# A hybrid attention and HGRN layer: down-weight differences formed beside the up tiles, a tile of their own for the meta rows, ScalarE first at query and key banks, three first-stage banks

## The chip, the cores and the metric

The kernel runs on one core of a Trainium2 chip, in one launch. The metric is the device time of that launch in microseconds (us). The engines of the core work from queues of their own: TensorE (PE; its weight loads are PEld), VectorE (DVE), ScalarE (ACT), GpSimd (POOL) and SyncE (SP), which only issues transfers here.

## The reference

One decoder layer over 1024 tokens with 16 meta tokens ahead of them (1040 rows), width 1024, in float32. Two kinds of heads work side by side on the same input, four differential-attention heads and four HGRN2 heads; a convolutional feed-forward layer follows.

```python
a = rmsnorm(h, ln_mix_pre[l])
proj = a @ w_in[l]
dq, dk, dv, hq, hf, hi, hg = jnp.split(proj, SPLITS, axis=-1)
...
y_diff = diff_attention(dq, dk, dv, diff_lambda[l], diff_subln[l], rel_bias_table, lam_init)
y_hgrn = hgrn2(hq, hf, hi, hg, lb_all[l], hgrn_gnorm[l])
mix = jnp.concatenate([y_diff, y_hgrn], axis=-1) @ w_out[l]
h = h + rmsnorm(mix, ln_mix_post[l])
a = rmsnorm(h, ln_ffn_pre[l])
y = conv_ffn(a, w_ffn_up[l], ffn_conv_w[l], ffn_conv_b[l], w_ffn_down[l])
h = h + rmsnorm(y, ln_ffn_post[l])
```

`conv_ffn` multiplies by a 1024 x 5632 matrix, convolves each of the 5632 channels over three tokens, multiplies gelu of one half by the other half and multiplies by a 2816 x 1024 matrix. The meta rows are dropped from the output.

## The kernel before

Every float32 operand of a large matmul is split into a high part (rounded to the matmul's input type) and a low part (the rest), and each product is three matmuls: high x high, high x low, low x high. `split` (L146) makes the parts: a ScalarE cast, then a subtraction on VectorE or GpSimd.

The order of TensorE's instructions is the order of the program (`manual_schedule`, L104). On the other engines, and on SyncE's queue of transfers, a planner orders the instructions: among those whose inputs its model of the time finds ready, it takes the one that comes first in the program. So an operation can be put far ahead of its place in the text when nothing holds it back. `issue_after(x)` keeps an operation behind x on x's engine, and while `state["ordered"]` is set (L792 to L907) the other engines keep program order too. A tile with a tag takes one of the tag's buffers; a further tile of the tag waits until a buffer is released.

The stages, in order of time:

1. **First stage** (L756 to L923, about the first 60 us). Nine blocks of rows are normed, transposed on TensorE and stored as `ahi` and `alo`. Between the transposes stand the query, key and value projections of head 0, for three groups of blocks (`GROUPS`, L31). `head0_first` (L849) gives the matmuls of the first group piece by piece, `block` (L889) transposes one block, `far_block` (L838) prepares one. PSUM has 8 banks: two with the tag `ip`, six with the tag `m` (`deep`, L110). `bias_tables` (L304) forms the lambda term `nlam` and then the bias tables of the four heads.
2. **Heads** (L935 to L940). For each head, `interleave` (L59) mixes two streams: the HGRN projections (`dense`, L742) with attention (`attn`), then the next head's query, key and value projections with the HGRN recurrence (`hgrn_head`). A projection group ends in an evacuation: `ev_q` (L594) and `ev_k` (L599) write a query or key bank as high part in one half of the partitions and low part or a copy in the other. `flush` (L391) transposes value tiles that an earlier group left; `dense` calls it in step 8 of the 24 of a group. `dense` also draws one step of `down_sums` (L184) per group: it loads four 128x512 blocks of the down weights for each of 11 row blocks, forms four differences on VectorE (S11 = W12 - W11, S12 = W22 - W12, S22 = W22 - S11, S21 = W21 - S22, in place) and stores them in the scratch array `tsc`. The tiles have the tag `wd`, six buffers of the pool `wdsums`.
3. **Output projection and norms** (L942 to L1253). Its first half of the columns is made beside the last HGRN head, its second half in a loop over blocks (L1218). `post` (L1131) of a block loads its residual rows `xh` (two buffers), adds the normed output, stores the sum in `hsc` and norms it again; `trans(i - 2)` transposes an earlier block on TensorE. The meta rows are block 0: their `xh` is also what `trans(0)` reads, in iteration 4.
4. **Up projections** (L1339 to L1372). For 22 column tiles `ft`, each with two halves of the tokens, the 2 x 2 block product is made from seven products in place of eight (`unit`, L1298: steps j = 0 to 6). After j = 1, the addition `u2` reads the bank pb, into which step 3 accumulates further. `gated` (L1272) convolves on ScalarE and VectorE, multiplies on GpSimd and stores a tile in `gsc`. `prep` (L1083) makes the weights' sums and parts for the next tile, from tiles `ra`.
5. **Down projection** (L1374 to L1547). The same seven-product scheme; four of its weight operands are the differences that lie in `tsc` (L1397), the others come from the weights themselves. Its operands from `gsc` are loaded into tiles with the tag `gk` (L1390), four buffers of the pool `down`, which opens at L1359, ahead of the up tiles.

Of the kernel before, what the change touches and what calls it, by code (L numbers as in the profile page):

```python
# [33 lines left out]
FA, FH, FO = 840, 800, 740  # L34

# [50 lines left out]
def layer_kernel(ctx: ExitStack, tc: tile.TileContext, x, meta, table, lbl, gpre, gpost, win,  # L86
# [23 lines left out]
    deep = {"ip": 2, "m": 6}  # L110
# [73 lines left out]
    def down_sums():  # L184
        def load(k):
            with tc.issue_after(last_load[-1].ins):
                for nm, kk, half in (("11", k, 0), ("12", k, 1), ("22", k + NF // 2, 1), ("21", k + NF // 2, 0)):
                    b[nm] = wsp.tile([P, 512], F32, tag="wd", name=f"wd{nm}_{k}")
                    SY.dma_start(b[nm], wdown[P * kk: P * (kk + 1), 512 * half: 512 * (half + 1)])

        b = {}
        load(0)
        yield
        yield
        for k in range(NF // 2):
            for j, d, p_, q_ in ((0, "11", "12", "11"), (2, "12", "22", "12"), (1, "22", "22", "11"), (3, "21", "21", "22")):
                V.tensor_tensor(b[d], b[p_], b[q_], op=ALU.subtract)
                with tc.issue_after(last_load[-1].ins):
                    SY.dma_start(tsc[j][P * k: P * (k + 1)], b[d])
                yield  # L200
            if k + 1 < NF // 2:
                load(k + 1)
                yield

    wd_sums = down_sums()
# [98 lines left out]
    def bias_tables():  # L304
# [8 lines left out]
        V.tensor_scalar(nlam, nlam, -(0.8 - 0.6 * math.exp(0.0)), None, ALU.add)  # L313
        oh = zp.tile([32, 384], F32, tag="oh", name="oh", bufs=1)
# [270 lines left out]
    def attn_in(h):  # L585
# [299 lines left out]
    def ahead_of(n):  # L885
        for _ in range(n):
            next(first_group)
# [726 lines left out]
```

## Time and profile before

| | us |
|---|---|
| three timed runs | 1338.4, 1341.98, 1343.84 |
| their median | 1341.98 |
| the profiled execution | 1336.17 |
| its span, first to last instruction | 1334.1 |
| busy ScalarE | 692.0 |
| busy GpSimd | 432.3 |

The profile is of one execution. All work of an engine that goes through the wrapper at L45 to L56 carries the line L53, so such instructions are known by their tiles: `u<-pb,x` is an operation that writes u from pb and x. Matmul durations overlap, since TensorE is pipelined; what counts is the distance from one start to the next. In a list of instructions in order of time, the columns are the start, the time taken, the engine, the line, the operation, the tiles, the shapes, and in brackets the idle time before it with what ended that.

### The profile page before, as it was taken

To read this page: it belongs to the slowest core of one execution; us is meant where nothing else is said; L and a number is where in the kernel's file an instruction comes from. 1 tells how busy PE (TensorE), PEld (TensorE's weight loads), DVE (VectorE), ACT (ScalarE), POOL (GpSimd) and SP (SyncE) were. 2 spreads that over 40 slices of the span, in tenths; PEclk is the share of its full clock that TensorE was granted. 3 is DMA by queue.
4 is the path that set the end of the run, shared out by engine and by line. 5 is a ranking of instruction groups with operands and counts; after the bars stand their busy time and mean duration, and the time that the engine had idled before them with its cause. 6 is when DMAs were issued, how large, how long until landed. Compare 5 with 4: busy or idle time off the path is not lost.

```text
span 1334.1 us, 26146 instructions
## 1 busy us (share of the span) xinstructions
PE 1287.9 (97%) x10172; PEld 1187.0 (89%) x10172; DVE 911.1 (68%) x1531; ACT 692.0 (52%) x1635; POOL 432.3 (32%) x340
## 2 busy tenths in 40 slices
PE   7999999999999999998998999999999999999997
PEld 6899899989999998677888999999999998878875
DVE  7675657475746574647797687787787776697586
ACT  8465356535654665246665445444445444454453
POOL 5211212121212110334055666666666630010121
PEclk9999999999999999999999999999999999999999
DMA  5331343144311223686412222223222226954253
GB/s 208 123 129 62 116 153 116 56 141 134 111 56 54 82 85 127 194 258 230 144 54 83 95 88 72 74 94 103 87 81 72 82 86 211 326 181 166 88 205 118
DMA packets 99425, 164.99 MB, mean 124 GB/s; under 512 B 10035, under 2 KB 34899, under 8 KB 99302
## 3 DMA queue, kind: packets, MB, share of 16 engines
q1 hardware_dynamic: 99302, 163.32, 35.9%
q8 instruction: 80, 1.31, 0.4%
q14 instruction: 43, 0.35, 0.1%
HBM read 122.65 MB, written 40.63 MB: 122 GB/s over the span
## 4 chain that ended last, share of the span: by engine, by line
PE 46%; DVE 7%; issue 3%; ACT 3%; DMA 2%; POOL 2%; SPq 0%; DVEq 0%; POOLq 0%; ACTq 0%
PE pd L1460 5%; PE pd L1461 5%; PE pd L1459 5%; PE pb L1309 4%; PE pb L1311 4%; PE pb L1310 4%; PE pc L1309 2%; PE pa L1309 2%; PE pa L1311 2%; PE pa L1310 2%; PE pc L1310 2%; PE pc L1311 2%; PE py L982 1%; PE py L980 1%; PE py L978 1%
## 5 line engine op out<-in xcount | busy, mean ns | idle before, releaser
L1309 PE MATMUL pb<-t,uh 128*128 128x258 f32 x504 | 142.9, 284 | 7.7 <-DVE u L53 7.7
L1310 PE MATMUL pb<-t,uh 128*128 128x258 f32 x504 | 141.7, 281 | 0.0
L1311 PE MATMUL pb<-t,ul 128*128 128x258 f32 x504 | 141.5, 281 | 0.0
L1460 PE MATMUL pd<-wl,gh 128*128 128x512 f32 x308 | 122.0, 396 | 0.3 <-DVE wl L53 0.2
L1459 PE MATMUL pd<-wh,gh 128*128 128x512 f32 x308 | 121.6, 395 | 0.0
L1461 PE MATMUL pd<-wh,gl 128*128 128x512 f32 x308 | 121.6, 395 | 0.0
L53 DVE SCALAR_TENSOR_TENSOR c<-uu,cwt,c 128x514 f32<-128x514 f32 (+1 forms) x88 | 97.1, 1104 | 20.6 <-ACT c L53 19.9
L1309 PEld LDWEIGHTS pb<-t,uh 128*128 128x128 f32 x504 | 95.4, 189 | 9.2 <-DVE u L53 8.9
L53 POOL TENSOR_TENSOR c<-c,c 128x514 f32<-128x514 f32 (+1 forms) x44 | 63.4, 1441 | 122.6 <-ACT c L53 118.5
L1310 PEld LDWEIGHTS pb<-t,uh 128*128 128x128 f32 x504 | 95.5, 189 | 0.0
L1311 PEld LDWEIGHTS pb<-t,ul 128*128 128x128 f32 x504 | 95.2, 189 | 0.0
L1309 PE MATMUL pa<-t,uh 128*128 128x258 f32 (+1 forms) x336 | 95.2, 283 | 0.0
L1311 PE MATMUL pa<-t,ul 128*128 128x258 f32 (+1 forms) x336 | 95.0, 283 | 0.0
L1310 PE MATMUL pa<-t,uh 128*128 128x258 f32 (+1 forms) x336 | 94.8, 282 | 0.0
L1309 PE MATMUL pc<-t,uh 128*128 128x258 f32 (+1 forms) x336 | 94.4, 281 | 0.0
L1310 PE MATMUL pc<-t,uh 128*128 128x258 f32 (+1 forms) x336 | 94.0, 280 | 0.0
L1311 PE MATMUL pc<-t,ul 128*128 128x258 f32 (+1 forms) x336 | 93.7, 279 | 0.0
L53 DVE SCALAR_TENSOR_TENSOR c<-ug,cwt,c 128x514 f32<-128x514 f32 (+1 forms) x88 | 86.7, 986 | 2.0 <-ACT c L53 1.4
L53 POOL TENSOR_TENSOR ul<-ws,uh 128x512 fp32r<-128x512 f32 x42 | 61.0, 1453 | 41.1 <-ACT uh L53 36.6
L1460 PEld LDWEIGHTS pd<-wl,gh 128*128 128x128 f32 x308 | 57.7, 187 | 15.5 <-DVE wl L53 1.6
L1459 PEld LDWEIGHTS pd<-wh,gh 128*128 128x128 f32 x308 | 57.7, 187 | 14.1
L1461 PEld LDWEIGHTS pd<-wh,gl 128*128 128x128 f32 x308 | 57.7, 187 | 14.0
(372 smaller groups left out, 4119.4 us busy)
## 6 DMA issues: line engine op xcount, KB each, us to landing
ra<-in_wup_dram SPq DMA_DIRECT2D x88, 256.0 KB, 2.6
mp<-msc SPq DMA_DIRECT2D x23, 512.0 KB, 6.3
wd<-in_wdown_dram SPq DMA_DIRECT2D x44, 256.0 KB, 4.4
tsc<-wd SPq DMA_DIRECT2D x44, 256.0 KB, 2.8
wi<-tsc SPq DMA_DIRECT2D x44, 256.0 KB, 2.8
gi<-gsc SPq DMA_DIRECT2D x33, 256.0 KB, 3.9
wi<-in_wdown_dram SPq DMA_DIRECT2D x33, 256.0 KB, 3.2
gsc<-c SPq DMA_DIRECT2D x22, 257.0 KB, 2.1
```

The lines of the kernel that those rows point to most:

```text
L53: ins = call(*args, **kw)
L978: T.matmul(py[:r], mh, hi, start=(first and k == ks[0]), stop=False)
L980: T.matmul(py[:r], mh, lo, start=False, stop=False)
L982: T.matmul(py[:r], ml, hi, start=False, stop=(last and k == ks[-1]))
L1309: T.matmul(pt, hi[:, s], th[:, k], start=(first and k == 0), stop=False, skip_group_check=True)
L1310: T.matmul(pt, hi[:, s], tl[:, k], start=False, stop=False, skip_group_check=True)
L1311: T.matmul(pt, lo[:, s], th[:, k], start=False, stop=(k == 3), skip_group_check=True)
L1459: T.matmul(py, gh[:, s], wh, start=(k == 0 and pr not in (3, 7)), stop=False, skip_group_check=True)
L1460: T.matmul(py, gh[:, s], wl, start=False, stop=False, skip_group_check=True)
L1461: T.matmul(py, gl[:, s], wh, start=False, stop=(k == NH - 1), skip_group_check=True)
```

## The change

It has these parts:

- `down_sums` moves from the projections to the up tiles, into the pool `down` with the tag `gk`. From tile 6 on (`SUMS`) it is drawn once after each of the steps j = 1, 3, 5 and 6, behind the newest addition that reads a bank of `unit` (`marks["last"]`). Its loads have no such tie.
- `xh` of the meta rows goes into the tile e0 of the pool `early`, and the loads of `xh` are issued one block earlier, after the loads of the next block's operands.
- `ev_q` and `ev_k`: ScalarE's reads of a bank come first, then VectorE's; the copy of the key's high part to the other partitions reads the copy in SBUF, not the bank.
- `flush` in `dense` at step 14, not 8.
- First stage: three `ip` banks and five `m` banks. The first group's matmuls are written out by kind; the query bank is evacuated after block 4, the key bank after block 5, and the query bank of the second group is filled between the value parts. The second value weights are split after block 3. The lambda term goes behind the last `alo` part, together with the small tables.

```diff
-    deep = {"ip": 2, "m": 6}
+    deep = {"ip": 3, "m": 5}
...
         def ev_q(g, b0, b1, t0, t1, pt):
             for m in range(2):
                 A.mul(qs[m][own[m], t0:t1], pt[own[m]], 0.125)
+            for m in range(2):
                 V.scalar_tensor_tensor(qs[m][oth[m], t0:t1], pt[own[m]], 0.125, qs[m][own[m], t0:t1].bitcast(F32), ALU.mult, ALU.subtract)
 
         def ev_k(g, b0, b1, t0, t1, pt):
             for m in range(2):
                 A.copy(ks[m][own[m], t0:t1], pt[own[m]])
+            for m in range(2):
                 V.tensor_tensor(kl[m][own[m], t0:t1], pt[own[m]], ks[m][own[m], t0:t1].bitcast(F32), op=ALU.subtract)
-                A.copy(ks[m][oth[m], t0:t1], pt[own[m]])
+            for m in range(2):
+                A.copy(ks[m][oth[m], t0:t1], ks[m][own[m], t0:t1].bitcast(F32))
...
-                next(side, None)
                 for step, c in enumerate(proj_group(g, parts, name, evac)):
-                    if step == 8:
+                    if step == 14:
                         flush()
...
-    ahead_of(32)
+    dq, dk = Kinds(0, 0, ps_in), Kinds(1, 0, ps_in)
+    dq.part(0, 0, ahi, True)
+    dk.part(0, 0, ahi, True)
+    dq.part(0, 1, ahi)
+    dq.part(0, 0, alo)
+    dk.part(0, 0, alo)
+    dk.part(0, 1, ahi)
+    dq.part(1, 0, ahi)
+    dk.part(1, 0, ahi)
     block(3)
     load_x(8)
+    third_hi(1)
     far_block(5)
     for c in range(2):
-        G.tensor_tensor(third[c][:, 1], raws[2, c], third[c][:, 0].bitcast(F32), op=ALU.subtract)
-        parts[2][c] = third[c][:, 0], third[c][:, 1]
-    ahead_of(16)
+        third_lo(c)
+    dq.part(1, 0, alo)
+    dq.part(1, 1, ahi, False, True)
+    dk.part(1, 0, alo)
+    dk.part(1, 1, ahi, False, True)
     block(4)
-    ahead_of(16)
+    dv = Kinds(2, 0, ps_m)
+    for half in range(2):
+        dv.part(half, 0, ahi, not half)
+    dq.out()
+    for half in range(2):
+        dv.part(half, 0, alo)
     last_hi, last_lo = block(5)
-    ahead_of(8)
+    dk.out()
+    dv.part(0, 1, ahi)
+    dq = Kinds(0, 1, ps_in)
+    for half in range(2):
+        dq.part(half, 0, ahi, not half)
+    dv.part(1, 1, ahi, False, True)
+    dv.out()
+    for half in range(2):
+        dq.part(half, 0, alo)
+    for half in range(2):
+        dq.part(half, 1, ahi, False, half)
+    dq.out()
     state["ordered"] = False
...
-    interleave(head0(1), [pre_blocks([6, 7, 8])], 3600, 1800)
+    interleave(head0(1), [pre_blocks([6, 7, 8])], 2400, 0)
     with tc.issue_after(last_lo.ins):
         smalls()
+        lam_terms()
     interleave(head0(2), [bias_tables()], 2600)
...
+    def load_xh(i):
+        r = tok(i)[0]
+        if i:
+            xhs[i] = qp.tile([P, D], F32, tag="xh", name=f"xh{i}")
+        else:
+            xhs[i] = ep.tile([P, D], F32, tag="e0", name="xh0")
+        SY.dma_start(xhs[i][:r], meta[14:16, :] if i == 0 else x[P * (i - 1): P * i, :])
...
-        xh = qp.tile([P, D], F32, tag="xh", name=f"xh{i}")
-        SY.dma_start(xh[:r], meta[14:16, :] if i == 0 else x[P * (i - 1): P * i, :])
+        xh = xhs.pop(i)
...
+        if i == 1:
+            load_xh(1)
+            load_xh(0)
         if i + 1 < NBLK:
             second_load(i + 1)
+            load_xh(i + 1)
...
+    def down_sums():
+        for k in range(NF // 2):
+            b = {}
+            for nm, kk, half in (("11", k, 0), ("12", k, 1), ("22", k + NF // 2, 1), ("21", k + NF // 2, 0)):
+                b[nm] = dn.tile([P, 512], F32, tag="gk", name=f"wd{nm}_{k}")
+                SY.dma_start(b[nm], wdown[P * kk: P * (kk + 1), 512 * half: 512 * (half + 1)])
+            yield
+            for j, d, p_, q_ in ((0, "11", "12", "11"), (2, "12", "22", "12"), (1, "22", "22", "11"), (3, "21", "21", "22")):
+                V.tensor_tensor(b[d], b[p_], b[q_], op=ALU.subtract)
+                SY.dma_start(tsc[j][P * k: P * (k + 1)], b[d])
+                yield
...
     for ft in range(1, NF):
         units = [unit(ft, p, ps_b) for p in range(2)]
         for j in range(7):
             prep(7 * (ft + 1) + j)
             for u in units:
                 next(u)
+            if ft >= SUMS and j in (1, 3, 5, 6):
+                with tc.issue_after(marks["last"].ins):
+                    next(wd_sums, None)
```

`Kinds(j, g, bank)` holds the bank of projection j (0 query, 1 key, 2 value) of group g; `part(half, w, a)` gives four matmuls of one half of the contraction with the weights' high (0) or low (1) part and `ahi` or `alo`; `out()` evacuates the bank. `third_hi(c)` and `third_lo(c)` make the value weights' parts. `lam_terms` is what stood first in `bias_tables`.

More of the change, by code (lines that the diff above doesn't have):

```diff
@@ L182, in layer_kernel @@
     last_load = []
[L184 to L205, printed above, removed]
     at_p_cm, ap_ = pool("attn", 1, "right")
@@ L883, in layer_kernel, with third_lo, __init__, part @@
-    first_group = head0_first()
-    def ahead_of(n):
-        for _ in range(n):
-            next(first_group)
+        parts[2][c] = third[c][:, 0], third[c][:, 1]
+    def third_lo(c):
+        G.tensor_tensor(third[c][:, 1], raws[2, c], third[c][:, 0].bitcast(F32), op=ALU.subtract)
+    third_hi(0)
+    class Kinds:
+        def __init__(self, j, g, bank):
+            self.j, self.g = j, g
+            self.t0, self.t1 = start(GROUPS[g][0]), start(GROUPS[g][1] - 1) + P
+            self.pt = bank(f"pi_{tiles[j][1]}_{g}")[:, : self.t1 - self.t0]
+        def part(self, half, w, a, first=False, last=False):
+            for k in range(4 * half, 4 * half + 4):
+                T.matmul(self.pt, parts[self.j][half][w][:, P * (k % 4): P * (k % 4 + 1)], a[:, k, self.t0:self.t1],
+                         start=bool(first and k == 0), stop=bool(last and k == KD - 1))
+        def out(self):
+            tiles[self.j][2](self.g, *GROUPS[self.g], self.t0, self.t1, self.pt)
```

54 lines of the change are left out of this document (15 added, 39 removed).

## The prediction

> **What bounds the kernel now.** I read the page first, then the whole-span waits of the matmul engine, then windows and timelines at the places which these waits name.
>
> ```profile
> span 1334.1 us, 26146 instructions
> PE 1287.9 (97%) x10172; PEld 1187.0 (89%) x10172; DVE 911.1 (68%) x1531; ACT 692.0 (52%) x1635; POOL 432.3 (32%) x340
> ```
>
> TensorE is busy 97% of the span, and the change neither adds nor removes a matmul. So each edit can only shorten or lengthen TensorE's own waits. Those are few:
>
> ```profile
> PE pb L1309 <- DVE u L53: 7.7, 6, 3.3
> PE pl L442 <- DVE hq L53: 7.3, 5, 1.8
> PE pa L1171 <- DVE a L53: 3.8, 2, 3.5
> PE pi_dv L224 <- ACT k L53: 2.5, 3, 1.5
> ...
> PE pi_dq L226 <- DVE alo L53: 1.6, 1, 1.6
> ...
> PE pn_vh L338 <- ACT pb L53: 1.2, 1, 1.2
> PE pn_vh L338 <- ACT ona L53: 1.0, 3, 0.3
> PE pi_dv L857 <- POOL w L53: 1.0, 2, 0.6
> ...
> PE pn_va L338 <- ACT vt L53: 0.6, 1, 0.6
> ```
>
> Each row gives total us, number of waits and the longest one. Nearly all these waits are on VectorE or ScalarE results that come late, and most of the edits aim at one of these rows. The exception is the stage to which the down-weight differences move, the up projections, where TensorE waits for nothing. There the question is how much room VectorE has left.
>
> **Part 1, the differences leave the projections.** There are 44 of them with 44 loads and 44 stores:
>
> ```profile
> L189 SPq DMA_DIRECT2D wd<-in_wdown_dram x44: 333/430/1192, 50.4 to 342.2; - x44
> L53 DVE TENSOR_TENSOR wd<-wd,wd x44: 673/693/1716, 56.4 to 349.8; 128x512 f32<-128x512 f32 x44
> L199 SPq DMA_DIRECT2D tsc<-wd x44: 320/411/1138, 57.1 to 376.8; - x44
>   DMA wd<-in_wdown_dram: 8.7, 10
> ```
>
> They end at 349.8 us, and that is a natural experiment. The stretch from the first query matmul of the next head to its first HGRN matmul runs three times, twice with eight differences and once with none:
>
> ```profile
> 137.80:191.30 53.50, 50.31 (x732) 47.52 (x732) 33.89 (x67) 23.84 (x67) 10.44 (x12) 1.00 0.36 120
> 267.10:321.10 54.00, 50.34 (x732) 47.50 (x732) 34.83 (x67) 23.81 (x67) 11.01 (x12) 1.00 0.35 118
> 397.20:447.90 50.70, 50.13 (x733) 47.44 (x732) 28.54 (x59) 23.83 (x67) 9.86 (x12) 1.00 0.18 57
> ```
>
> Columns: the stretch, its length, then busy us (and count) of PE, weight loads, DVE, ACT, POOL. TensorE's work is the same (732 weight loads each), VectorE's is 67, 67 and 59 instructions, and the lengths are 53.5, 54.0 and 50.7. Removing the differences is therefore worth 2.8 + 3.3 = 6.1 us. The other half of each head (attention beside HGRN projections) shows no such step, so I count nothing there. I take **-6.1**; bounds -9 (all waits on hq and a little more) and 0.
>
> **Part 2, evacuation order and later flush.** Query banks now get both ScalarE multiplies before both VectorE differences, key banks both casts first, and the last two key copies read SBUF, not the bank. The bank is released one or two engine hand-overs earlier. The row on k has three waits, 2.5 us; the longest (1.5) lies inside the first stretch above and is counted already, the other 1.0 goes. A copy from SBUF costs no more than one from the bank within the noise of this sum, and ScalarE is 24 us busy in a 51 us stretch, which hides it. Flushing value transposes at step 14, not 8, gives their source copy six more matmuls. The three pn rows (1.2, 1.0, 0.6: 2.8 us) lose most, say 2.5. Together **-3.5**; bounds -5.3 (all of both) and +1 (a transposed value block is late for its own reader).
>
> **Part 3, first stage.** Here is what holds the first 384-wide group:
>
> ```profile
> 24.72 1.73 DVE L53 TENSOR_TENSOR lv<-lv 128x64 f32<-128x64 f32 x2
> ...
> 27.07 2.48 DVE L53 TENSOR_TENSOR alo<-px,ahi 128x512 fp32r<-128x512 f32 x4
> ```
> ```profile
> 29.01 0.44 PE L226 MATMUL pi_dq<-alo,wh_dq 128*128 128x384 f32 x1 [1.65 <-DVE alo L53]
> ```
>
> The lambda products (lv) and what follows them occupy VectorE from 24.72 to 27.07, ahead of the four alo parts for which TensorE waits 1.65. They move behind the last alo. Moreover the query bank of the second group gets a third bank and starts between the value parts, so it fills that time. The two waits on w (1.0) stay in part, because the GpSimd order ahead of them (far_block(5)) is the same. One bank fewer for transposes may cost something. I take **-2**; bounds -3.5 (alo, w and the rest of that stretch) and +1.
>
> **Part 4, the residual rows.** Around block 3 of the second output half:
>
> ```profile
> 618.98 0.81 SPq L1134 DMA_DIRECT2D xh<-in_x_dram  x2
> ```
> ```profile
> 623.63 0.75 DVE L53 SCALAR_TENSOR_TENSOR xh<-y,ssy,xh 128x512 f32<-128x512 f32 x1 [3.48 <-DMA xh<-in_x_dram]
> ```
> ```profile
> 629.18 1.97 PE L1171 MATMUL pa<-ident,a 128*128 128x128 f32 x8 [3.48 <-DVE a L53]
> ```
> ```profile
> 620.00:640.00 20.00, 16.52 (x69) 13.34 (x69) 10.29 (x13) 11.67 (x30) 1.39 (x2) 0.83 0.71 251
> ...
> 660.00:680.00 20.00, 20.00 (x171) 20.00 (x170) 19.02 (x18) 17.21 (x28) 0.66 (x1) 1.00 0.07 27
> ```
>
> The meta rows hold one of the two xh buffers until their transpose in iteration 4, so block 3's rows are only requested at 618.98, when block 2 is done; VectorE waits 3.48 for them and TensorE 3.48 after that. The granted clock of this window is 0.83, and the eight transposes took 1.97 us. Missing clock of 0.17 x 20 = 3.4 us, about half of it outside the idle gap, puts the whole stall at 5 to 6.4. With a tile of their own for the meta rows and the request one block ahead, these rows are there before block 3 is summed. Next late is VectorE itself, whose chain gains its own 3.48 but is 19 of 20 us busy from 660 on. I take **-5**; bounds -6.4 and 0.
>
> **Part 5, what the moved loads displace.** The differences use the four `gk` buffers, which today are taken by operands of the down stage, pulled forward into the first up tiles:
>
> ```profile
> 701.33 0.62 ACT L53 CAST gh<-gi 128x512 fp32r<-128x512 f32 x1 [5.29 <-DMA gi<-gsc]
> ```
> ```profile
> 701.99 0.69 DVE L53 TENSOR_TENSOR gl<-gi,gh 128x512 fp32r<-128x512 f32 x1 [3.50 <-ACT gh L53]
> ```
> ```profile
> 700.00:720.00 20.00, 16.70 (x141) 16.50 (x140) 13.29 (x20) 9.64 (x18) 10.08 (x8) 1.00 0.28 102
> 720.00:740.00 20.00, 19.55 (x164) 19.23 (x163) 15.98 (x23) 9.10 (x17) 12.25 (x9) 1.00 0.27 93
> ...
> 900.00:920.00 20.00, 20.00 (x171) 20.00 (x170) 14.93 (x22) 9.73 (x17) 13.60 (x10) 1.00 0.23 79
> ```
>
> ScalarE stands 5.29 us in front of a load that needs a store just made, VectorE 3.50 behind it, and TensorE gets 141 and 164 matmuls into windows where steady state has 171: 37 x 0.117 = 4.3 us. The first difference loads have no producer, so they take the four buffers as soon as the pool opens, and the operands come after the last difference, one or two tiles before the down stage, with their data long stored. I take **-4**; bounds -5.2 (two more tiles like the second) and 0.
>
> **Part 6, the differences beside up tiles.** From tile 6, four of 55 steps per tile (44 differences, 11 loads): 13.75 tiles, 3.2 differences each, issued behind the newest addition at j = 1, 3, 5 and 6. A steady tile takes 20 us, and VectorE does this in it:
>
> ```profile
> 903.75 0.87 DVE L53 TENSOR_TENSOR ul<-ra,uh 128x512 fp32r<-128x512 f32 x1 [2.53 <-ACT uh L53]
> ...
> 906.68 0.42 DVE L53 TENSOR_TENSOR uu<-pb,x 128x256 f32<-128x256 f32 x1
> 907.01 1.53 DVE L53 SCALAR_TENSOR_TENSOR c<-uu,cwt,c 128x514 f32<-128x514 f32 x1
> ...
> 911.62 0.42 DVE L53 TENSOR_TENSOR ug<-pc,u 128x256 f32<-128x256 f32 x1
> ...
> 913.21 2.45 DVE L53 SCALAR_TENSOR_TENSOR c<-ug,cwt,c 128x510 f32<-128x510 f32 x2
> ...
> 916.19 0.75 DVE L53 TENSOR_TENSOR u<-pb,x 128x258 f32<-128x258 f32 x2
> 918.03 1.47 DVE L53 TENSOR_TENSOR ul<-ws,uh 128x512 fp32r<-128x512 f32 x1 [1.10 <-ACT uh L53]
> ```
> ```profile
> 917.24 0.29 PE L1309 MATMUL pb<-t,uh 128*128 128x258 f32 x1
> ```
> ```profile
> 913.53 1.58 POOL L53 TENSOR_TENSOR c<-c,c 128x514 f32<-128x514 f32 x1 [3.83 <-ACT c L53]
> ```
>
> The steps at j = 1 and j = 3 meet idle time (1.10 before 918.03, 2.53 before 903.75), so they cost nothing; without that cover each would cost its 0.69. The steps at j = 5 (behind 906.68) and j = 6 (behind 911.62) fall into a stretch without idle time that ends with the u2 additions at 916.19. Queued behind them are the convolutions and these additions, and for the additions TensorE waits before it may accumulate into the same bank at 917.24. The first of the pair ends near 916.55, so 0.7 us are spare. Of every five tiles, three have a difference at both steps and two at one. At p us for each, a tile loses 2p - 0.7 or p - 0.7. The row of wd has a median of 0.69 and a maximum of 1.72; I take p = 0.8, near the median, as GpSimd stands idle for 3.83 us of that stretch (before 913.53): 0.9 x 8.25 + 0.1 x 5.5 = **+8**. Bounds: 0 (all in idle time) and, at 1.72, 2.74 x 8.25 + 1.02 x 5.5 = +28. The 88 DMAs move into SyncE's queue ahead of weight loads (ra) and gate stores; at 0.4 us each they add 2.6 us of issue to a 20 us tile, hidden unless a store waits for its difference and the next ra load stands behind it, which would show within the upper bound.
>
> A rule of the Trainium skill speaks against this part: the page "SBUF — State Buffer", section "SBUF: two separate sides", says that VectorE with two SBUF inputs and a GpSimd operation that reads SBUF hold a shared port pair exclusively, so that the later one waits for the other's end. The trace leans that way: in the same kind of operation 0.69 and 1.4 us both occur. By that rule, and what it gives, see the second rival.
>
> **Sum.** -6.1 - 3.5 - 2 - 5 - 4 + 8 = -12.6 us. The profiled execution took 1336.17 (span 1334.1 and 2.1 around it), which becomes 1323.6. The three timed runs have a median 5.8 above it, 1341.98, so their figure becomes **1329**.
>
> **The rivals.**
> *The differences are free*: the order puts all of them into the two idle gaps, which are long enough for 3.2 x 0.69 = 2.2 us. For it: 3.6 us idle against 2.2. Against it: two of four steps are bound to additions inside the dense stretch. -20.6, 1321.
> *They meet GpSimd*: GpSimd is busy 13.6 of 20 us in the steady window, so two starts in three wait for the rest of an operation, and p is 1.2: 1.7 x 8.25 + 0.5 x 5.5 = 17 instead of 8, net -3.6, 1338. Against it: GpSimd's gap lies in this very stretch.
> *Slower*: VectorE becomes the bound in the up tiles. The loss per tile is 1.6p - 0.7 and the gains of 20.6 are 1.5 per tile, so from p = 1.4 on the change loses. At the 1.72 that the row of wd shows as its worst, it is +28 - 20.6 = +7.6, 1350. For it: 14.93 busy of 20 plus 3.2 x 1.72 is more than 20. Against it: the median is 0.69.
> *It does not do what it says in the middle*: the down operands still take their buffers first, and the post-norm chain is held by VectorE rather than by loads. Parts 4 and 5 fall out: -6.1 - 3.5 - 2 + 8 = -3.6, 1338. For it: VectorE's 19.02 busy from 660 to 680.
>
> **Chances.** Forecast 0.48, free 0.15, GpSimd 0.15, slower 0.12, middle 0.10. About 0.5%, 6.7 us, is what a measurement can tell from no change. Below 1335.3 lie 0.45 of the forecast's 0.48, the free case, and about half of the two cases at 1338: 0.71. Slower than 1348.7 is most of the third rival: 0.10. Between them 0.19. The range runs from the free case with a little more gain, 1315, to the foot of the slower case, 1346.
>
> **What would show it.** Part 1: the three stretches have one length, near 50.7. Part 2: the rows on k and pn shrink. Part 3: no wait on alo before 30 us. Part 4: no wait of L1171 on a, and a full clock from 620 to 640. Part 5: no gh cast near 700 us. Part 6: a new repeated wait of pb on u, 0.2 to 1.2 us per tile, from the seventh up tile to about the twentieth, and none after. The prediction is wrong if these waits exceed 1.5 us per tile, or if the up tiles from 6 on are as long as before.

## The result, and the profile after

| | before | after |
|---|---|---|
| median of 13 runs each, us | 1341.47 | 1334.53 |
| lowest to highest | 1336.26 to 1346.11 | 1330.96 to 1337.41 |
| profiled execution, us | 1336.17 | 1334.41 |
| its span | 1334.1 | 1332.6 |

The ratio is 0.9957, 95% interval 0.9943 to 0.997: 0.43% faster, or 5.8 us of 1341. The two medians lie 6.9 us apart. Either is about half of the 12.6 us forecast. The time lies inside the range (1315 to 1346), 5.5 us above the figure of 1329. The two profiled executions differ by less (1.5 us of span) than the medians (6.9 us), since that of before lay at the low end of its runs.

The page of the kernel after, its first lines and the groups of up matmuls (columns: line, engine, operation, tiles, shape, count, then busy us and mean ns, then the idle time before and what ended it). Lines of the helper are now L54, those of the up products L1316 to L1318.

```profile
span 1332.6 us, 26191 instructions
...
PE 1288.0 (97%) x10172; PEld 1187.6 (89%) x10172; DVE 931.6 (70%) x1531; ACT 692.5 (52%) x1635; POOL 456.2 (34%) x340
...
L1316 PE MATMUL pb<-t,uh 128*128 128x258 f32 x504 | 144.8, 287 | 11.9 <-DVE u L54 11.8
```

TensorE's work is the same to 0.1 us, and so is the number of VectorE's instructions, but VectorE is 20.5 us busier (931.6 against 911.1) and GpSimd 23.9 (456.2 against 432.3): the same work takes longer where it now stands. The whole-span waits of TensorE (total us, count, longest):

```profile
PE pb L1316 <- DVE u L54: 11.8, 13, 3.5
PE pn_vh L319 <- ACT pb L54: 5.8, 3, 2.5
...
PE pn_va L317 <- ACT kn L54: 1.9, 3, 0.6
...
PE pl L417 <- DVE hq L54: 1.4, 1, 1.4
...
PE pa L1174 <- DVE a L54: 1.0, 2, 0.8
```

The waits of pl on hq fell from 7.3, those of pa on a from 3.8, and those on k and alo are gone. The wait of pn_vh on pb grew from 1.2 to 5.8, where it was to shrink, and that of pb on u from 7.7 to 11.8. The three query-key-value stretches and the last two HGRN stretches of the kernel after (columns as in the prediction):

```profile
133.70:184.50 50.80, 50.13 (x733) 47.45 (x733) 28.97 (x59) 24.12 (x68) 9.93 (x12) 1.00 0.18 51
260.80:311.50 50.70, 50.03 (x733) 47.36 (x732) 28.95 (x59) 24.11 (x67) 9.93 (x12) 1.00 0.17 51
387.90:438.60 50.70, 50.03 (x732) 47.35 (x731) 28.95 (x59) 24.11 (x67) 9.94 (x12) 1.00 0.19 56
311.50:387.90 76.40, 73.42 (x506) 71.39 (x506) 43.34 (x100) 46.40 (x138) 12.55 (x11) 1.00 0.16 46
438.60:517.20 78.60, 74.94 (x506) 72.70 (x506) 45.01 (x104) 47.92 (x141) 10.10 (x8) 0.98 0.28 89
```

Stage by stage, from the starts of the stages' first matmuls in both profiles:

| stage | before | after | difference | forecast |
|---|---|---|---|---|
| to the first HGRN matmul | 61.6 | 59.7 | -1.9 | -2 |
| three query-key-value stretches | 158.2 | 152.2 | -6.0 | -6.1 |
| four HGRN stretches | 304.0 | 305.3 | +1.3 | -3.5 with the next row |
| first output half (py to pz) | 72.3 | 74.0 | +1.7 | |
| second half (pz to pq) | 58.8 | 53.6 | -5.2 | -5 |
| up tiles 1 to 6 | 129.4 | 122.8 | -6.6 | -4 |
| up tiles 7 to 19 | 259.1 | 268.5 | +9.4 | +8 |
| up tile 20 | 19.9 | 25.3 | +5.4 | 0 |
| all the rest | 270.8 | 271.2 | +0.4 | 0 |

Five rows came near the forecast or better. Two did not: the HGRN stretches with the first output half (+3.0 where -3.5 stood), and up tile 20, for which the prediction counts nothing. Here is the place in the first of them, in the kernel after: ScalarE's and TensorE's instructions near the end of the last head's attention, in order of time.

```profile
487.99 0.49 ACT L54 COPY ht<-pi_hi 128x384 f32<-128x384 f32 x1
...
489.58 0.38 PE L694 MATMUL pa<-avn,az 128*128 128x128 f32 x2
...
489.80 1.50 PE L694 MATMUL pa<-avn,at 128*128 128x128 f32 x12
...
492.67 0.70 ACT L54 ACTIVATE pb<-S,ast 128x528 f32<-128x528 f32 x1 [2.29 <-DVE ast L54]
...
493.36 0.68 ACT L54 ACTIVATE pb<-E,ast 128x512 f32<-128x512 f32 x1
...
494.19 0.90 PE L319 MATMUL pn_vh<-ident,ht 128*128 128x128 f32 x3 [2.53 <-ACT pb L54]
```

The transposes' source, ht, is done at 488.5. They start at 494.19, just behind the exponential that reads the score tile E. So they do not wait for their data but for a bank: they draw from the `m` banks, of which there are two from the attention stage on (`deep.update(ip=2, m=2)`, L920), and the one with E is free only when VectorE has found its maximum and ScalarE has read it. That it is the bank is read from the order of these rows and the code; no run gives the transposes a bank of their own. In the kernel before the same three transposes stand ahead of pa:

```profile
499.13 0.55 PE L338 MATMUL pn_vh<-ident,ht 128*128 128x128 f32 x3 [0.32 <-ACT ona L53]
500.25 0.49 PE L710 MATMUL pa<-avn,az 128*128 128x128 f32 x2
```

And up tile 20 of the kernel after, first as a window, then instructions of ScalarE, VectorE and TensorE in it:

```profile
1060.80:1086.20 25.40, 21.93 (x171) 21.61 (x170) 20.73 (x30) 12.51 (x22) 12.02 (x8) 0.93 0.49 159
```
```profile
1062.28 0.63 ACT L54 CAST gh<-gi 128x512 fp32r<-128x512 f32 x1 [1.82 <-DMA gi<-gsc]
...
1064.16 0.62 ACT L54 CAST gh<-gi 128x512 fp32r<-128x512 f32 x1 [0.73 <-DMA gi<-gsc]
1064.68 0.81 ACT L54 ACTIVATE c<-uu,cbt,cwt 128x510 f32<-128x510 f32 x1
```
```profile
1065.60 1.12 DVE L54 SCALAR_TENSOR_TENSOR c<-uu,cwt,c 128x510 f32<-128x510 f32 x1 [2.42 <-ACT c L54]
...
1072.50 0.41 DVE L54 TENSOR_TENSOR u<-pb,x 128x258 f32<-128x258 f32 x1
```
```profile
1072.97 0.39 PE L1316 MATMUL pb<-t,uh 128*128 128x258 f32 x1 [3.47 <-DVE u L54]
```

The first down operands come as soon as the last difference gives the `gk` buffers free. ScalarE stands 1.82 and 0.73 us before two of their loads, with a step of the convolution behind them. VectorE stands 2.42 us for that step, then works without a gap and reaches the addition for u at 1072.50, and TensorE has waited 3.47 us for it. That is all of the idle time in the tile: 21.93 us of matmul in 25.4. The other 2.0 us over a steady tile are matmuls further apart: the granted clock is 1.00 up to the wait and 0.63 from 1073 to 1077 us, right behind it.

### The profile page after: what moved, and what is told of

It reads as the page before. It is cut to its first block, busy times and chain, and to the rows that moved or that the text cites. A ratio compares the mean times of both kernels' runs of the same rounds, so it can differ in the third digit from the quotient of the medians.

```text
span 1332.6 us, 26191 instructions
## 1 busy us (share of the span) xinstructions
PE 1288.0 (97%) x10172; PEld 1187.6 (89%) x10172; DVE 931.6 (70%) x1531; ACT 692.5 (52%) x1635; POOL 456.2 (34%) x340
## 4 chain that ended last, share of the span: by engine, by line
PE 43%; DVE 10%; DMA 4%; issue 3%; ACT 3%; POOL 1%; SPq 0%; DVEq 0%; ACTq 0%; POOLq 0%
PE pd L1484 5%; PE pd L1483 5%; PE pd L1485 5%; PE pb L1316 4%; DVE c L54 3%; PE pb L1317 3%; PE pb L1318 3%; PE pa L1316 2%; PE pa L1317 2%; PE pa L1318 2%; PE pc L1316 2%; PE pc L1317 2%; PE pc L1318 2%; DMA gi<-gsc 1%; DVE ul L54 1%
## 5 line engine op out<-in xcount | busy, mean ns | idle before, releaser
L1316 PE MATMUL pb<-t,uh 128*128 128x258 f32 x504 | 144.8, 287 | 11.9 <-DVE u L54 11.8
L1318 PE MATMUL pb<-t,ul 128*128 128x258 f32 x504 | 142.3, 282 | 0.0
L54 POOL TENSOR_TENSOR c<-c,c 128x514 f32<-128x514 f32 (+1 forms) x44 | 74.9, 1702 | 120.6 <-ACT c L54 110.3
L1316 PEld LDWEIGHTS pb<-t,uh 128*128 128x128 f32 x504 | 96.1, 191 | 15.2 <-DVE u L54 15.0
L54 DVE SCALAR_TENSOR_TENSOR c<-uu,cwt,c 128x514 f32<-128x514 f32 (+1 forms) x88 | 87.6, 1004 | 22.6 <-ACT c L54 22.3
L1318 PEld LDWEIGHTS pb<-t,ul 128*128 128x128 f32 x504 | 95.9, 190 | 0.0
L1316 PE MATMUL pa<-t,uh 128*128 128x258 f32 (+1 forms) x336 | 95.2, 283 | 0.0
L1318 PE MATMUL pa<-t,ul 128*128 128x258 f32 (+1 forms) x336 | 95.0, 283 | 0.0
L1316 PE MATMUL pc<-t,uh 128*128 128x258 f32 (+1 forms) x336 | 94.4, 281 | 0.0
L1318 PE MATMUL pc<-t,ul 128*128 128x258 f32 (+1 forms) x336 | 93.7, 279 | 0.0
L54 DVE SCALAR_TENSOR_TENSOR c<-ug,cwt,c 128x514 f32<-128x514 f32 (+1 forms) x88 | 88.2, 1002 | 1.5 <-ACT c L54 1.4
L54 ACT CAST uh<-ra 128x512 fp32r<-128x512 f32 x67 | 41.0, 616 | 67.9 <-PE pb L1317 49.7
L54 POOL TENSOR_TENSOR ul<-ws,uh 128x512 fp32r<-128x512 f32 x42 | 63.8, 1519 | 27.1 <-ACT uh L54 27.1
```

Source lines behind the costliest of these rows:

```text
L54: ins = call(*args, **kw)
L1316: T.matmul(pt, hi[:, s], th[:, k], start=(first and k == 0), stop=False, skip_group_check=True)
L1318: T.matmul(pt, lo[:, s], th[:, k], start=False, stop=(k == 3), skip_group_check=True)
```

## The experiments

Each is given with its median, its ratio to the kernel before of the same chip (95% interval) and what its profile shows. A tile's length is the distance from its first pa matmul to the next tile's.

**The flush back at step 8, the rest as after** (`flush8_in_after`).

```diff
-                    if step == 14:
+                    if step == 8:
                         flush()
```

> The changed kernel with its value transposes flushed at step 8 again, all else kept. Theory: at step 14 the transposes stand behind the score and value matmuls of the other stream, the two m banks are taken by a score tile E and by pa, and TensorE waits for the exponentials that release E (5.8 us in three waits on pn_vh, 1.9 on pn_va). With step 8 the three waits on pn_vh fall below 1.5 us in all, the HGRN stretches of heads 1 to 3, now 76.3, 76.4 and 78.6 us, come back to about 75.7, and the span is 4 to 6 us shorter than the changed kernel's 1332.6. Rival: the new evacuation order of the query and key banks shifted ScalarE's queue, and the flush step has no part in it; then the stretches stay above 76 us and the span within 1 us.

1327.1 us, 0.9893 (0.9865 to 0.9922), span 1324.3, 8.3 less than after. TensorE's waits and two of the same stretches:

```profile
PE pb L1316 <- DVE u L54: 12.3, 13, 4.2
...
PE pn_vh L319 <- ACT ona L54: 1.0, 3, 0.3
```
```profile
308.90:384.20 75.30, 73.64 (x506) 71.33 (x505) 42.43 (x100) 46.58 (x138) 12.56 (x11) 1.00 0.15 48
434.10:511.20 77.10, 74.17 (x505) 71.22 (x504) 44.90 (x104) 47.85 (x141) 9.84 (x8) 1.00 0.29 91
```

Of the waits of pn_vh on pb one of 0.6 us is left, and those of pn_va on kn (1.9 us after) are gone. The HGRN stretches give back 3.5 us in sum, the query-key-value stretches 2.5 (49.9 each), the first output half 1.6. It is more than the expected 4 to 6, since the step also stands in the projections of the next head.

**The flush at step 14 in the kernel before** (`flush14_in_before`): the same edit the other way, nothing else changed.

> The kernel before with nothing changed but the flush at step 14. Theory of the bank: waits on pn_vh grow from 2.2 us to 5 or more, waits on pn_va appear in the query-key-value stretches, and the span grows by 3 to 6 us over 1334.1, 0.2 to 0.5 per cent slower. What the prediction said of it: the pn waits (2.8 us) lose 2.5 and the kernel becomes that much faster. Rival (evacuation order is the cause): no change either way.

1345.52 us, 1.0031 (1.0015 to 1.0047), span 1344.4. The wait appears by itself:

```profile
PE pn_vh L338 <- ACT pb L53: 5.9, 3, 2.5
```

In both directions the later step costs time: 0.0031 of 1341 us or 4.2 us here, (0.9957 - 0.9893) x 1341 = 8.6 us in the pair above. The prediction had it gain 2.5.

**All steps of the differences moved into the two gaps, two at a time** (`gap_steps_in_after`).

```diff
-            if ft >= SUMS and j in (1, 3, 5, 6):
-                with tc.issue_after(marks["last"].ins):
-                    next(wd_sums, None)
+            if ft >= SUMS and j in (1, 3):
+                for _ in range(2):
+                    with tc.issue_after(marks["last"].ins):
+                        next(wd_sums, None)
```

> The changed kernel with the four steps per up tile drawn as two behind j = 1 and two behind j = 3, where VectorE had 1.10 and 2.53 us idle, and none behind j = 5 and 6. Theory 1 (place): the loss comes from the stretch without idle time ahead of the u2 additions; tiles 7 to 19, which lost 9.4 us in the changed kernel against 19.93 each, lose less than 3. Theory 2 (load beside GpSimd): a difference takes 1.39 us in the median there, because GpSimd holds it up wherever it stands, and GpSimd is busier around j = 1 and 3; the loss stays at 8 us or grows. Both expect tile 20 to stay near 25 us.

1349.18 us, 1.0064 (1.0044 to 1.0084), span 1349.4: (1.0064 - 0.9957) x 1341 = 14 us slower than after. Tiles 7 to 19 are 20.0 to 23.7 long and lose 24.7 us against 19.93 each, where after loses 9.4, and tile 20 is 27.05. Here, on VectorE, the pair behind step 3 of the tile that starts at 902.2, and then a window of the tile behind it:

```profile
913.99 0.41 DVE L54 TENSOR_TENSOR u<-pb,x 128x258 f32<-128x258 f32 x1
...
915.57 3.27 DVE L54 TENSOR_TENSOR wd<-wd,wd 128x512 f32<-128x512 f32 x2
918.76 1.78 DVE L54 TENSOR_TENSOR ul<-ra,uh 128x512 fp32r<-128x512 f32 x1
920.46 0.42 DVE L54 TENSOR_TENSOR uu<-pb,x 128x258 f32<-128x258 f32 x1
```
```profile
922.30:943.90 21.60, 20.21 (x170) 20.01 (x169) 20.05 (x26) 9.38 (x17) 13.80 (x9) 1.00 0.55 174
```

Two differences take 3.27 us, not 1.4, and VectorE, 14.93 of 20 us busy before, is 20.05 of 21.6 busy: the pair is longer than the idle time, and everything behind it comes late. So "in the gap" is not free by itself. Whether one in each gap is, the last three experiments ask.

**The early down operands held back in the kernel before** (`late_operands_in_before`): the casts and low parts of the first four are issued behind the last up tile's first x1 cast and u2 addition, and the first has no priority.

```diff
-            with tc.high_priority() if i == 0 else nullcontext():
+            if i < 4:
+                with tc.issue_after(marks["act"].ins), tc.issue_after(marks[NF - 1, 1].ins):
+                    ready[i] = operands(*steps[i])
+            else:
                 ready[i] = operands(*steps[i])
```

> The kernel before, with the casts and low parts of the first four down-stage operands held behind the first cast and the first addition of the last up tile (no high priority for the first). Theory: ScalarE's wait for the load of an operand just stored, in front of everything else, is what makes up tiles 2 to 5 long (24.21, 20.85, 20.83, 20.11 us); they come to about 20.1, 19.93, 19.93, 19.93, and 5 to 6 us go from the span; the last tile grows by 0 to 2 us for four low parts in a row. Rival: tile 2 is long because VectorE is behind with convolutions from tile 1, and stays above 23 us; the gain is below 2.5 us.

1333.56 us, 0.9934 (0.9903 to 0.9964). Tiles 2 to 5 are 20.07, 19.93, 19.93, 19.93 in place of 24.21, 20.85, 20.83, 20.11: the stall is gone, and the last tile, up to the first down product, keeps its 19.94. This one edit is worth about as much as the whole change (the intervals overlap), without moving a difference. That the span of its profile, 1335.2, is not below 1334.1 lies ahead of the tiles: its first up tile starts 7.5 us later than before's, of which the stretches of the heads took 5.5, and the edit touches none of what lies there.

**The differences back beside the projections, the rest as after** (`sums_back_in_after`). The generator and its calls in `dense` are those of the kernel before, the call in the up tiles is gone.

> The kernel after, with the 44 differences back beside the projections as in the kernel before; evacuation order, flush step 14, first stage and residual rows stay as after. It separates the move itself (Parts 1, 5, 6) from the order of evacuations. Theory 1 (the differences were what lengthened the query-key-value stretches): these go back from 50.8, 50.7, 50.7 to about 53.5, 54, 50.7 (+6.0); up tiles 7 to 19 go back to 19.93 each (-9.4); tile 20 goes from 25.33 to 19.93 (-5.4); tiles 1 to 6 get back what they lost to early down operands (+6.6, tile 2 near 24.2). Net -2.2, span about 1330 against 1332.6. Rival (the new evacuation order is what shortened these stretches, the differences did nothing there): they stay at 50.7, span about 1324.

1337.96 us, 0.9972 (0.9956 to 0.9989), span 1331.0. Its three query-key-value stretches and a steady up window:

```profile
134.50:186.90 52.40, 50.29 (x733) 47.47 (x732) 34.72 (x67) 24.12 (x67) 9.94 (x12) 1.00 0.39 123
264.80:319.40 54.60, 50.47 (x734) 47.53 (x733) 35.75 (x67) 24.11 (x67) 10.99 (x12) 1.00 0.38 119
397.80:448.50 50.70, 50.03 (x732) 47.36 (x731) 28.96 (x59) 24.11 (x67) 9.93 (x12) 1.00 0.19 55
926.00:946.00 20.00, 20.00 (x171) 20.00 (x170) 15.06 (x25) 9.62 (x17) 13.62 (x10) 1.00 0.24 80
```

The stretches with eight differences are 1.6 and 3.9 us longer than after's, the one without is the same: the differences made them long, not the order of evacuations. Tiles 7 to 20 are 19.93 each; tile 2 is 24.41. The HGRN stretches differ as well: the first three, with eight differences each, take 4.5 us more here than after, the fourth, which has none, 1.5 less. So the move as a whole is worth little: by these two profiles it gains 5.5 us in the query-key-value stretches, 3.0 in the HGRN stretches and 6.4 in the first up tiles, and loses 9.4 and 5.4 in the later ones and 1.7 elsewhere. Without it the span is 1.6 us shorter, but the ratio is 0.0015 higher (2 us) and the intervals overlap; the profiled execution is the fastest of ten here.

**The residual rows alone, in the kernel before** (`rows_only_in_before`): `load_xh` with its tile for the meta rows and its three calls, as in the diff.

> The kernel before with Part 4 alone: the meta rows get a tile of their own and each block's residual rows are requested one block ahead. Theory (VectorE's late rows were the stall): the stretch from the first z matmul to the first plain up product goes from 58.8 to about 53.6, span 5 shorter, ratio about 0.996; no other stretch changes. Rival (VectorE is full there and another part of the change brought that gain, the shorter queues on SyncE for instance): the stretch stays at 57 or more and the ratio is 0.999 to 1.001.

1336.44 us, 0.997 (0.9954 to 0.9987). The stretch from the first z matmul, in the kernel before and here:

```profile
596.10:654.90 58.80, 54.99 (x255) 44.51 (x254) 40.60 (x48) 36.96 (x111) 16.35 (x11) 0.94 0.63 225
```
```profile
602.20:656.10 53.90, 52.55 (x256) 42.33 (x255) 42.86 (x48) 37.37 (x111) 16.76 (x11) 1.00 0.69 241
```

It is 4.9 shorter, with the clock at 1.00 in place of 0.94. The ratio is near the expected 0.996. The span of this one profile, 1336.9, is longer than before's 1334.1 all the same, since other stretches took more: 2.4 us in the query-key-value stretches, 2.0 in the first output half, 2.2 in up tiles 1 to 6. That no other stretch would change did not hold for this execution.

**Flush at step 8 and the late operands, in the kernel after** (`flush8_late_operands`): both edits above.

> The kernel after with the flush back at step 8, and with the casts and low parts of the first four down operands held behind the last up tile's first cast and u2 addition. Theory (the 5.4 us of tile 20 are the early operands standing in front of a load of gates just stored, and nothing else): tile 20 goes from 25.9 to about 20.3, the last tile stays at 19.8, the down stage stays, so span about 1319 against 1324.3 and a ratio near 0.985. Rival (the operands are needed by then, so the same wait comes back at the first down products): the down stage is 3 to 5 us longer, span 1322 to 1324, ratio near 0.989.

1322.13 us, 0.9867 (0.9839 to 0.9895), span 1319.6. Tile 20 is 20.45 where `flush8_in_after` had 25.87, the last tile 19.94 as there. The span is 4.7 shorter. What lies behind the last tile is 0.9 longer (226.5 against 225.6), so of the 5.4 won little comes back: the operands are not needed earlier.

**The differences beside the HGRN projections** (`best`): as the last one, but two steps of the differences are drawn in every HGRN group and none elsewhere.

```diff
+                    if step in (0, 12):
+                        next(side, None)
                     if step == 8:
                         flush()
```

> As flush8_late_operands, but the differences go neither beside the query-key-value projections nor beside the up tiles: two of them in every group of the HGRN projections, where VectorE is busy 40 to 45 of 74 to 77 us and GpSimd 10 to 13 us. Theory (a difference costs only where VectorE's additions have no room beside GpSimd): up tiles 7 to 19 go back to 19.93 (-9.4), the HGRN stretches stay within 1 us of 74.1, 75.3, 75.3, 77.1, span about 1310 to 1312, ratio 0.977 to 0.981. Rival (a difference costs TensorE the same wherever it stands beside projections, 6.1 us for 16 or 0.38 each): the HGRN stretches become 16 us longer in sum, span about 1326, ratio 0.99.

1323.69 us, 0.9873 (0.9852 to 0.9895), span 1321.2, no gain on the last. The up tiles are 19.93 (tile 8 is 20.21), but the two stretches that hold most of the differences are 6.8 and 5.0 us longer:

```profile
59.70:140.60 80.90, 75.91 (x502) 73.41 (x501) 49.65 (x116) 44.77 (x135) 12.97 (x13) 0.96 0.43 138
190.90:271.20 80.30, 75.82 (x506) 71.30 (x506) 53.51 (x116) 45.73 (x139) 12.93 (x11) 1.00 0.45 143
```
```profile
66.89 0.69 DVE L54 TENSOR_TENSOR wd<-wd,wd 128x512 f32<-128x512 f32 x1 [4.40 <-DMA wd<-in_wdown_dram]
67.50 0.17 DVE L54 TENSOR_REDUCE ast<-S 16x2 f32<-16x32 f32 x1
```

The theory falls in its place: VectorE was 40 to 42 us busy in 74 to 75 there, and it still cost TensorE 11.8/32 = 0.37 us for each of the 32 differences that ran in these two stretches, the rival's 0.38. (Four ran ahead of them, and eight in the query-key-value stretches between and behind them, which are 1.0 longer in sum.) In part it is the first load, for which VectorE stood 4.40 us with a score reduction behind it. Busy shares say little of how much room a chain of short steps has.

**One difference in each gap** (`two_places`): as `flush8_late_operands`, but steps at j = 1 and 3 of every tile and at j = 6 in tiles 2 to 8, and the next loads in the step of the fourth difference.

```diff
-            if ft >= SUMS and j in (1, 3, 5, 6):
+            if j in (1, 3) or j == 6 and 2 <= ft <= 8:
```

> As flush8_late_operands, with the same 44 differences beside the up tiles but only in the two gaps: one behind the u2 additions (j = 1) and one behind the u3 additions (j = 3) of every tile from the first on, a third at j = 6 in tiles 2 to 8 alone; the next four loads are asked for in the step of the fourth difference. In the kernel after the tiles that carry a difference at j = 1 or 3 beside those at 5 and 6 are no longer than tiles without it, while two at each gap cost 1.6 us a tile. Theory (a gap takes one difference and no more): tiles 9 to 19 are within 0.15 us of 19.93, tiles 3 to 9 within 0.4, so span about 1312 against 1319.6 and a ratio of 0.979 to 0.982. Rival (VectorE beside GpSimd has no room at all, so a difference costs about 0.2 us wherever it stands): tiles 3 to 20 are 20.3 to 20.5 each, span 1319 to 1320, ratio 0.987.

1318.17 us, 0.9811 (0.9782 to 0.984), span 1317.5. Tiles 10 to 20, of which all but the last carry two differences, are 19.93, as without any. Tiles 3 to 9, which follow a third one at j = 6, are 20.5 to 20.7 (0.4 over 19.93 at most was expected), and tile 2 is 21.81. The span gains 2.1 and not 7, as the last HGRN stretch and the output projections, which the edit does not touch, took 3.1 more in this execution, and tile 2 and the seven tiles behind it lost 6 us.

**Three steps a tile from the second tile** (`three_places`): j = 1, 3 and 6.

> As flush8_late_operands, with the steps at j = 1, 3 and 6 of every tile from the second on (three a tile, five steps for four differences and a load as before), none at j = 5. Theory (only what stands in the stretch without idle time counts, and one there costs its 0.69 to 1.1 less the 0.7 to spare): the tiles behind a difference at j = 6 are 20.2 to 20.3, the others 19.93 to 20.0, net about 5 us lost over the tiles against 9.2, span about 1315. Rival (all places cost the same, 44 differences are 9 us in any order): the tiles lose 9 in sum, span 1319 to 1320.

1316.62 us, 0.9802 (0.977 to 0.9834), span 1316.0. Tiles with j = 1 and 3 filled and a difference at j = 6 are followed by a tile of 20.5, with one of the two gaps filled by 20.2, and without a difference at j = 6 by 19.93. In sum 6 us are lost. So a gap hides its difference altogether only where none is added at j = 6; beside one it costs 0.3.

**Two gaps, no step in tile 1** (`two_from_second`).

```diff
-            if j in (1, 3) or j == 6 and 2 <= ft <= 8:
+            if ft >= 2 and (j in (1, 3) or j == 6 and ft <= 7):
```

> As two_places, but with no step in tile 1, where VectorE also carries the plain unit's additions, and with the third step at j = 6 in tiles 2 to 7: the last difference falls into tile 20. Theory (in tile 1 there is no gap to fill, from tile 2 on each gap takes one): tile 2 goes from 21.81 back to 20.1, tiles 3 to 8 stay near 20.5, tiles 9 to 20 are 19.93, span 1313 to 1315, ratio 0.978 to 0.980. Rival (the loss of tile 2 is the first difference itself, wherever the first one stands): tile 3 becomes 21.8 in its place, span 1316 to 1318, ratio 0.981.

1314.67 us, 0.981 (0.979 to 0.9831), span 1314.0. Tile 2 is 20.11, tiles 3 to 8 are 20.2 to 20.5, tiles 9 to 20 are 19.93, though the last difference falls into tile 21, not 20. A steady window of it:

```profile
910.00:930.00 20.00, 20.00 (x170) 20.00 (x170) 18.71 (x25) 9.57 (x18) 13.81 (x9) 1.00 0.43 140
```

TensorE is busy throughout, with VectorE at 18.71 of 20 us. So the loss of tile 2 was not that of the first difference wherever it stands; tile 1, where VectorE is busy 21.7 of 23.0 us without one, has no room for it. This kernel and `three_places` are the fastest, some 25 us below before and 20 below after; the two cannot be told apart by their intervals.

## Why the prediction was right and wrong

Two steps failed: the later flush, booked as a gain, cost time, and the displaced down operands, booked as coming back at no price, cost a tile 5.4 us. Two of the terms that came out near the forecast did so in part by luck.

**Part 2, the flush: the first step that failed.** The prediction says that "Flushing value transposes at step 14, not 8, gives their source copy six more matmuls" and books 2.5 us of gain from the three pn rows. It took the waits of pn_vh to be waits for the source. The runs show a cost of 4.2 to 8.6 us in its place, by the two pairs. The transposes also need one of two banks, and six matmuls later the interleaved attention has put a score tile and its apply product into these. The row "pn_vh <- ACT pb" stood in the prediction: pb is not what the transposes read, nor is ona, so a releaser with another name than the source was the sign of a bank. Even the bound for this part, +1, was too narrow. With the flush left at step 8 the change makes the kernel 14.5 us faster by the medians (1341.61 to 1327.1) and 9.8 by the spans; without the 2.5 booked here, 10.1 was forecast.

**Part 2, the evacuation order.** The waits of pi_dv on k are gone after, as said; no run has the order alone, so its worth stays open. A hint is the third query-key-value stretch, which holds no differences in any of these kernels: with the flush at step 8 it is 50.7 in the kernel before and 49.9 in `flush8_in_after`, at step 14 51.4 in `flush14_in_before` and 50.7 after. The order can be these 0.7 to 0.8 us, but so can another part. The key copies that read SBUF took 0.51 us each in the median, those that read the bank 0.47.

**Part 1, the differences leave the projections.** Right in place and nearly in size: `sums_back_in_after` gives 5.5 of the forecast 6.1 back by this edit alone, so the argument from three stretches with 67, 67 and 59 VectorE instructions held. That the row of the table shows -6.0 is in part luck: the later flush adds 2.5 in the same stretches, and some 3 more are gone by other parts. The sentence that the HGRN stretches show no such step did not hold: eight differences in each of the first three cost 4.5 us there by the same pair, which the flush hid in the kernel after.

**Part 3, the first stage.** -1.9 against -2, and no wait on alo is left. No run takes it apart.

**Part 4, the residual rows.** -5.2 against -5, by itself -4.9. The rival in which VectorE holds the chain and the gain falls out did not come.

**Part 5, the displaced operands: the second step that failed.** Tiles 1 to 6 gained 6.6, more than the forecast 4, as the casts there were the whole stall. But the sentence that the operands come "with their data long stored" and so at no price failed: they came as soon as the buffers were free, in tiles 19 and 20, and ScalarE stood before their loads again. +5.4 were given back, which `flush8_late_operands` takes out with an order that holds them. The net is -1.2.

**Part 6, the differences beside the up tiles.** 9.4 us were lost where 8 stood, and by the mechanism that was named: TensorE waits before it may accumulate into pb for a u2 addition that is queued behind a difference. The sizes in that sum were off, and that it came near 8 is in part luck. Behind differences at j = 5 and 6 a tile takes 0.7 to 1.2 more, where 0.9 was forecast, behind one of them 0.3 to 0.5, where 0.1 was. The price p was not 0.8 but 1.16 in the mean (51.1 us for 44, the median 1.39), against 0.74 in the kernel before, and it goes by the place: 0.68 at j = 6, about 1.45 at j = 5, 1.1 or 1.4 at j = 1, mostly 1.57 at j = 3. The mean is the second rival's 1.2, yet the loss was not its 17. Part of a difference is made up by the convolutions behind it: those of uu take 0.75 + 2.11 + 0.74 = 3.60 us around the difference at 894.54 (last section), and 0.76 + 1.53 + 2.23 = 4.52 in the steady tile of the kernel before, where one of them stood beside GpSimd's operation in the place of the difference. Nor were 0.7 us spare: a difference at j = 6 alone takes 0.68 and costs 0.30. The gaps at j = 1 and 3 do hide one difference each where none stands at j = 6, and `two_places` shows this with 11 tiles of 19.93; two at once they do not hide.

**The sum and the median.** By its own profile the change was to be 12.6 and was 1.5. The gap of 11.1 is made of 6.5 in the HGRN stretches and the first output half (+3.0 for -3.5), 5.4 in tile 20, 1.4 in tiles 7 to 19 and 0.4 in the rest, less the 2.6 that tiles 1 to 6 brought over the forecast. The 5.8 us between before's profiled execution and its median were carried to after, where the two agree within 0.1. Before's 13 runs spread over 9.9 us, after's over 6.5. The stretches with differences are among what varies: in the profile of `rows_only_in_before`, which leaves them as before, they are 54.5 and 55.4 against 53.5 and 54.0, while the third, without differences, stays at 50.7. Whether that is all of it was not tried.

## What to carry to other kernels

Ask of a wait whose releaser is not the source of the waiting instruction which buffer or bank that releaser held, before a step is moved later; the later place may find the bank taken by a longer chain. When work is put into another's buffers, follow the displaced work to where it lands and give it an order of its own there. A gap on an engine has a size: fill it once with the duration that the operation has in that stage, not the one that it had elsewhere.

## What the runs showed of the hardware

The same 128x512 subtraction took 0.69 us in the median beside the projections and 1.39 beside the up tiles, where GpSimd is busy 13.6 of 20 us, both in the row for wd:

```profile
L54 DVE TENSOR_TENSOR wd<-wd,wd x44: 679/1386/1583, 784.7 to 1061.5; 128x512 f32<-128x512 f32 x44
```

A closer look at VectorE and GpSimd of the kernel after, in the same twelve microseconds:

```profile
894.54 1.46 DVE L54 TENSOR_TENSOR wd<-wd,wd 128x512 f32<-128x512 f32 x1
...
896.25 2.11 DVE L54 SCALAR_TENSOR_TENSOR c<-uu,cwt,c 128x514 f32<-128x514 f32 x2
...
901.26 0.68 DVE L54 TENSOR_TENSOR wd<-wd,wd 128x512 f32<-128x512 f32 x1
901.86 1.78 DVE L54 SCALAR_TENSOR_TENSOR c<-ug,cwt,c 128x510 f32<-128x510 f32 x1
...
905.44 1.10 DVE L54 TENSOR_TENSOR wd<-wd,wd 128x512 f32<-128x512 f32 x1
```
```profile
894.08 1.36 POOL L54 TENSOR_TENSOR ul<-ws,uh 128x512 fp32r<-128x512 f32 x1 [0.68 <-ACT uh L54]
...
900.86 2.24 POOL L54 TENSOR_TENSOR c<-c,c 128x514 f32<-128x514 f32 x1 [3.72 <-ACT c L54]
904.39 1.60 POOL L54 TENSOR_TENSOR c<-c,c 128x510 f32<-128x510 f32 x1 [1.29 <-ACT c L54]
```

The difference at 905.44 ends at 906.54: GpSimd's multiply ends at 905.99, and 0.55 later so does the difference. The one at 894.54 ends at 896.00, 0.56 behind the GpSimd operation that ends at 895.44. The one at 901.26 runs at its full 0.68, and GpSimd's multiply beside it takes 2.24, 0.66 more than the 1.58 of the steady window in the prediction; the convolution at 901.86 takes 1.78 beside that multiply, as in the steady window the second of the two at 913.21 (2.45 in sum) is long beside its own. In these rows either engine is longer by about the time for which the other was ahead of it. That is what the Trainium skill's page "SBUF — State Buffer", section "SBUF: two separate sides", says of a port pair held by one of the two at a time; the trace agrees in these durations.

Unexpected was also that the loss does not add up. In `two_from_second` VectorE is busy 18.71 of 20 us, 94%, and TensorE loses nothing; in the window of `gap_steps_in_after` it is busy 20.05 of 21.6, 93%, and TensorE stands 1.4 us: the place at which the queue is late counts, not its share.
